# Modulation units of a diffusion backbone: four matmuls of 256 columns on four column groups in place of two of 512 on two

## The chip, the core and the metric

The kernel runs on one core of a Trainium2 chip. The metric is the device time of one execution in microseconds (us): 1765.45 us, the median of three runs (1758.45 to 1767.54). TensorE is called PE here (PEld where it loads weights), VectorE DVE, ScalarE ACT, GpSimd POOL, SyncE SP. SP issues the loads and stores; SPq is its queue.

## What is computed

Two trunk layers work on 640 tokens of 1024 features: 128 context tokens and 512 latent ones. Each layer normalises its input, mixes tokens by three parallel branches (retention, SSD, RG-LRU), and then runs a gated MLP. Both halves of a layer are modulated by a vector that depends on the layer and on the stream (context or latent) alone:

```
sh1, sc1, g1, sh2, sc2, g2 = jnp.split(mod[:, None, :].astype(x.dtype), 6, axis=-1)
h = rmsnorm(x, p['norm1_g']) * (1.0 + sc1) + sh1
mix, new_states = mixer(h, states, p, pos)
x = x + g1 * mix
h = rmsnorm(x, p['norm2_g']) * (1.0 + sc2) + sh2
x = x + g2 * conv_ffn(h, p)
```

Here mod is silu(c) @ w_ada + b_ada, where w_ada has 1024 rows and 6144 columns for each layer. Only the product with w_ada changes; there are two rows of c, one for each stream.

## The kernel before

The products of tokens with weights are split in two: weights and features are each written as a high and a low part (wh, wl and h_hi, h_lo), and three matmuls take the place of one. `Stream` (line 373) loads the weights (tile raw, two buffers), ACT writes wh, and POOL or DVE writes wl. `fm_job` makes products whose output has features on the partitions, `sweep_job` products whose output has tokens there. These jobs stand in one list, the main stream.

The modulation of the first half of layer 0 is made at the start (`start`, tiles ar). The rest is made in five rounds by class `Ada` (line 597): a round covers 2048 columns of w_ada, and has 16 units. A unit is a load of 128 x 1024 weights (tile araw, 512 KB, two buffers) and the matmuls that multiply it with csil, the 128 x 32 piece of silu(c) in which two columns are in use. Since csil is only 32 columns wide, a matmul takes one of the four groups of 32 columns of the array, by its tile_position, and writes 32 partitions of a PSUM tile. Even units (hf = 0) write groups 0 and 1, odd ones (hf = 1) groups 2 and 3. After the sixteenth unit, `finish` (line 643) adds the bias (tile rows), stores the gate's part to DRAM (grow), transposes rows, and writes the shift and the scale.

The order of all instructions is set while the program is built. Everything else (retention, SSD, RG-LRU, norms, `finish`) is a thread that is stepped when its inputs should be there, by a clock of estimated times (class `Clock`, line 60, and `Engine.account`, line 181). The engines run their instructions in the order that comes out. A unit is placed in one of three ways: in `run` (line 349), where the main stream has nothing to issue by that clock; in `Stream.done` (line 411), where more units are left than the rest of the phase should hold; or in `need` (line 682), where the round is due. `run` of Ada returns false as long as the unit's load has not landed by that clock. For the matmuls of a unit the clock has these lines:

```
cost = n * (4 if f32 and fn == "matmul" else 1) / 2400 + 0.003
...
if tp is not None and tp[1] > 0:
    cost = 0.02
```

So a matmul on the first column group is booked by its columns, and one on another group at a small flat price. An even unit is booked dear, an odd one at almost nothing.

In the rows of an order below, a unit is `at<-araw,csil`; `h_hi,wh` and the like are products of the main stream; `ident,tok` and `ident,C` are transposes; `X,wg` are the gates of the RG-LRU (their weights are tile wg); `C`, `pv,C` and `xs,tok` are the SSD's output for one tile of 128 tokens.

Of the kernel before, what the change touches and what calls it, by code (L numbers as in the profile page):

```python
# [59 lines left out]
class Clock:  # L60
    """estimated times of the engines, for the order in which instructions are emitted"""
# [10 lines left out]
    def windows(self, t):  # L72
        """the tensor engine's clock: how busy the last window was sets the rate of the next"""
        while t >= (self.win + 1) * HAM:
            u = self.busy / HAM
            self.cold = u < 0.85 if self.cold else u < 0.33
            self.busy = 0.0
            self.win += 1
# [32 lines left out]
    def free(self, n):  # L111
        """when the last user of a tile is done"""
        return max([r for r in self.read.get(n, {}).values()] + [self.ready.get(n, (0.0,))[0]])
# [20 lines left out]
def tnames(xs):  # L134
    """what the waits go by: tiles, or the rows of the tiles that are worked on in parts"""
    res = []
    for x in xs:
        n = getattr(getattr(x, "tensor", x), "name", None)
        w = ROWS.get(n.rsplit("_", 1)[0]) if n else None
        if w and not n.startswith(SHARED):  # L140
            ap = [(abs(st), c) for st, c in list(x.ap)[1:]]
            o = x.offset
            res += [f"{n}#{r}" for r in range(o // w, (o + sum(st * (c - 1) for st, c in ap)) // w + 1)]
        elif tname(x):
            res.append(n)
    return res


class Slots:
    """a pool whose tiles take over the waits of the tiles that had their place"""  # L150
# [92 lines left out]
def kernel(ctx: ExitStack, tc: tile.TileContext, a: dict, o: dict):  # L243
# [27 lines left out]
    # PSUM tiles and token-major tiles are taken and given back in emission order, so that no engine waits for a later one  # L271
# [91 lines left out]
    def pick(after=0.0, **cost):  # L363
        """the engine that would be through first"""
        return min(cost, key=lambda e: max(clk.t[e], clk.now() - 1.0, after) + cost[e])

# [1 line left out]
    def slot_free(tag, bufs):  # L368
        """when the next tile of the tag is free"""
        L = strm.names.get(tag, [])  # L370
        return clk.free(L[-bufs]) if len(L) >= bufs else 0.0

    class Stream:
        """units of the products' weights: loads run NRAW ahead of the splits, splits tn.look ahead of the products"""
# [56 lines left out]
    def load_x(key, src):  # L431
        """the residual stream stays out of SBUF while the mixer needs the room"""
        pl.enter("xp", key, side="right")
        x[:] = [pl["xp"].tile([128, D], F32, tag=f"x{t}", name="x") for t in range(5)]
        for t in range(5):
            SP.dma_start(x[t], src[t])
# [22 lines left out]
    def softplus(out, xin, n):  # L459
        """max(x, 0) + log1p(exp(-|x|)), log1p through 2 atanh(e / (2 + e))."""  # L460
        e, d, s2, acc = (small(n, f"sp{i}{n}", 1) for i in range(4))
        ACT.activation(e, xin, AF.Abs)
        ACT.activation(e, e, AF.Exp, scale=-1.0)
        yield
        DVE.tensor_scalar(d, e, 2.0, None, ALU.add)
        DVE.reciprocal(d, d)
        DVE.tensor_tensor(e, e, d, ALU.mult)
        DVE.tensor_tensor(s2, e, e, ALU.mult)
        DVE.tensor_scalar(acc, s2, 1.0 / 17.0, 1.0 / 15.0, ALU.mult, ALU.add)
        for c in (13.0, 11.0, 9.0, 7.0, 5.0, 3.0, 1.0):  # L470
            DVE.tensor_tensor(acc, acc, s2, ALU.mult)
            DVE.tensor_scalar(acc, acc, 1.0 / c, None, ALU.add)
        DVE.tensor_tensor(acc, acc, e, ALU.mult)
        DVE.tensor_scalar(d, xin, 0.0, None, ALU.max)
        DVE.scalar_tensor_tensor(out, acc, 2.0, d, ALU.mult, ALU.add)
# [9 lines left out]
    def setup():  # L485
        """log-gates of the retention (l, dir, h), softplus(-lambda) (l, dir, chunk), decay tables"""
# [30 lines left out]
    def fm_job(then, rev=False):  # L517
        """feature-major chunk: then(ps) gives the thread that consumes it"""
        ps = yield from get("mm", 2)
        w = ws.take()  # L520
        for n in range(8):
            for piece in range(2):
                fm_piece(ps, w, (7 - n if rev else n,), piece, 7 if rev else 0)
            if n == 7:
                ws.done()
                spawn(consume(then, ps), 0)
            yield
# [4 lines left out]
    def fm_primed(thens):  # L532
        """some chunks, the columns of the first tiles before the others"""
# [27 lines left out]
    def sweep_job(ks, ncol, ah, al, then, ready=None, keep=None):  # L561
        """token-major product over the k's, units of two k's; then(t, ps) consumes tile t"""
# [32 lines left out]
    mods = {}  # L595

    class Ada:
        """a unit: one k, two slices of 512 of the columns 2048 r .., to rows (32 j + stream)"""
# [19 lines left out]
        def left(self, due):  # L618
            """units up to the round that is due"""
            return max(0, 16 * (1 + ((0, 1), (0, 2), (1, 0), (1, 1), (1, 2)).index(due)) - self.n_run)  # L620

        def run(self):
            """the next unit, if that keeps nobody waiting"""
            if not self.got or clk.ready[tname(self.got[0])][0] > clk.now():
                return False
            l, r, k, hf = self.units[self.n_run]
            if k == 0 and hf == 0:
                if self.busy or not can("at", 1, 2):
                    return False
                self.busy = True  # L630
                self.rows = const.tile([128, 512], F32, tag="rows", name="rows")
                SP.dma_start(self.rows, a["bada"][l, r])
                self.ps, = now_(get("at"))
            raw = self.got.pop(0)
            for j in (2 * hf, 2 * hf + 1):
                PE.matmul(self.ps[32 * j:32 * j + 32, :], csil[:, k, :], raw[:, 512 * (j % 2):512 * (j % 2) + 512],
                          start=(k == 0), stop=(k == 7), tile_position=(0, 32 * j))
            self.n_run += 1
            if k == 7 and hf == 1:
                spawn(self.finish(l, r, self.ps, self.rows))  # L640
            return True

        def finish(self, l, r, ps, rows):
# [3 lines left out]
            if r > 0:  # L647
                j0 = 0 if r == 1 else 2
                dr = dram.tile([2, 1024], F32, tag="grow", name="grow", bufs=4)
                for jj in range(2):  # L650
                    p = 32 * (j0 + jj)
                    SP.dma_start(dr[:, 512 * jj:512 * jj + 512], rows[p:p + 2, :])
# [5 lines left out]
            v = pt.rearrange("p (q j s) -> p q j s", q=4, j=4)  # L658
            which = 0 if r == 0 else 1
            if r < 2:  # L660
                sh = mods["sh", l, which] = const.tile([128, 8, 2], F32, tag=f"sh{which}", name="sh")
                for jj in range(2):
                    DVE.tensor_copy(sh[:, 4 * jj:4 * jj + 4, :], v[:, :, 2 * r + jj, 0:2])
            if r != 1:
                s = const.tile([128, 8, 2], F32, tag=f"s{which}", name="s")
                for jj in range(2):
                    DVE.tensor_scalar(s[:, 4 * jj:4 * jj + 4, :], v[:, :, (2 if r == 0 else 0) + jj, 0:2], 1.0, None, ALU.add)
# [14 lines left out]
    def need(due):  # L682
        """the rounds up to this one, done"""
# [84 lines left out]
    def conv(dst, ps, w, right, rel_):  # L768
        """dst[c] = b + sum_j w[j] ps[c + j - 1]"""
# [17 lines left out]
    def lru(l, c, X, Y, done):  # L787
# [4 lines left out]
        for d in range(2):  # L792
# [22 lines left out]
            DVE.scalar_tensor_tensor(T, r, 1.0, T, ALU.add, ALU.mult)           # 1 - a = (1 + a) tanh  # L815
            DVE.scalar_tensor_tensor(r, T, 2.0, T, ALU.subtract, ALU.mult)      # a^2 - 1
            yield
            ACT.activation(r, r, AF.Sqrt, scale=-1.0)
            ACT.activation(T, T, AF.Identity, scale=-1.0, bias=1.0)             # a
# [36 lines left out]
    def ssd_dt(l, S):  # L856
        """dt, cumulative log-decays and their exponentials, token-major [128, tile, dir, h]"""
# [36 lines left out]
    def ssd_decay(l, S, t):  # L894
        """E[g][m, hh, i]: decay both ways, weighted by dt[m]"""
# [29 lines left out]
    def ssd_state(l, S, C, t):  # L925
        """token-major xs; the states that the chunk leaves, [n, g, (dir, hh, p)]"""
# [105 lines left out]
    def ssd_turn(l, S, t):  # L1032
        """feature-major, with the gain"""
# [33 lines left out]
    def rope_do(raw, t):  # L1067
        """raw -> rotated token-major tile"""
# [186 lines left out]
    def begin_phase(due):  # L1255
        """the modulation that is due at the end of the phase is spread behind its units"""
# [652 lines left out]
```

## Time and profile before

| | |
|---|---|
| runs, median (lowest to highest) | 1765.45 us (1758.45 to 1767.54) |
| profiled execution, own time: its span from first to last instruction | 1752.2 us |
| PE busy | 1661.6 us, 95% |
| DVE, ACT, POOL busy | 1009.3, 718.5 and 537.4 us |
| units of the modulation: PE busy | 53.2 us, between 92.8 and 1197 us |
| granted TensorE clock, mean | 0.982 |

No other time is known for the profiled execution than its span; the median of the runs is 13.2 us above it. A busy time counts the stretch from the start of a matmul to its modelled end, and matmuls are pipelined, so what a matmul costs is read from the start of one to the start of the next. A matmul of plain f32 operands, as the units' are, has two records in the trace; an order has it once.

### The profile page before, as it was taken

To read this page: it belongs to the slowest core of one execution; us is meant where nothing else is said; L and a number is where in the kernel's file an instruction comes from. 1 tells how busy PE (TensorE), PEld (TensorE's weight loads), DVE (VectorE), ACT (ScalarE), POOL (GpSimd) and SP (SyncE) were. 2 spreads that over 40 slices of the span, in tenths; PEclk is the share of its full clock that TensorE was granted. 3 is DMA by queue.
4 is the path that set the end of the run, shared out by engine and by line. 5 is a ranking of instruction groups with operands and counts; after the bars stand their busy time and mean duration, and the time that the engine had idled before them with its cause. 6 is when DMAs were issued, how large, how long until landed. Compare 5 with 4: busy or idle time off the path is not lost.

```text
span 1752.2 us, 25505 instructions
## 1 busy us (share of the span) xinstructions
PE 1661.6 (95%) x10192; PEld 1485.5 (85%) x10192; DVE 1009.3 (58%) x1866; ACT 718.5 (41%) x1136; POOL 537.4 (31%) x344
## 2 busy tenths in 40 slices
PE   6897999999999999999999899999899999999997
PEld 5787878768997999799789876887799989998996
DVE  5467987677443344344464779877854434443445
ACT  6466435426332233223274765443453313331333
POOL 1334653322331233123123355442213212321331
PEclk9998999999999999999999999999999999999999
DMA  8424555533223222322533355643122321222222
GB/s 326 121 49 81 128 179 174 187 109 103 73 73 108 64 82 73 96 73 73 180 121 107 75 135 158 181 166 105 60 73 73 87 81 61 73 85 72 73 85 84
DMA packets 62668, 188.63 MB, mean 108 GB/s; under 512 B 9550, under 2 KB 17734, under 8 KB 62550
## 3 DMA queue, kind: packets, MB, share of 16 engines
q1 hardware_dynamic: 62550, 187.01, 34.7%
q8 instruction: 80, 1.31, 0.3%
q14 instruction: 38, 0.31, 0.1%
HBM read 180.46 MB, written 6.52 MB: 107 GB/s over the span
## 4 chain that ended last, share of the span: by engine, by line
PE 72%; DVE 14%; ACT 4%; DMA 4%; issue 3%; POOL 1%; SPq 0%; POOLq 0%; DVEq 0%; ACTq 0%
PE at L175 72%; DVE tok L175 5%; DVE x L175 2%; DMA wg<-in_wlru 2%; DVE gt L175 1%; DVE sp L175 1%; DVE C L175 1%; DMA tok<-cTd 1%; ACT L175 1%; DVE lb L175 1%; ACT xn L175 1%; ACT hf L175 1%; POOL wl L175 1%; DMA araw<-in_w_ada 1%; ACT lb L175 1%
## 5 line engine op out<-in xcount | busy, mean ns | idle before, releaser
L175 POOL TENSOR_TENSOR wl<-raw,wh 128x1024 fp32r<-128x1024 f32 (+3 forms) x167 | 388.3, 2326 | 946.7 <-ACT wh L175 883.2
L175 PE MATMUL at<-h_hi,wh 128*128 128x258 f32 (+2 forms) x1912 | 599.9, 314 | 5.0 <-ACT wh L175 3.9
L175 PE MATMUL at<-h_hi,wl 128*128 128x258 f32 (+2 forms) x1912 | 590.4, 309 | 5.6 <-POOL wl L175 4.8
L175 PE MATMUL at<-h_lo,wh 128*128 128x258 f32 (+2 forms) x1912 | 590.0, 309 | 0.5 <-DVE h_lo L175 0.5
L175 PEld LDWEIGHTS at<-h_hi,wh 128*128 128x128 f32 x1912 | 363.7, 190 | 20.1 <-issue 5.2
L175 PEld LDWEIGHTS at<-h_hi,wl 128*128 128x128 f32 x1912 | 362.8, 190 | 6.9 <-POOL wl L175 5.9
L175 PEld LDWEIGHTS at<-h_lo,wh 128*128 128x128 f32 x1912 | 364.1, 190 | 2.6 <-DVE h_lo L175 0.7
L175 ACT ACTIVATE wh<-raw 128x1024 fp32r<-128x1024 f32 (+3 forms) x210 | 212.7, 1013 | 223.1 <-PE at L175 168.1
L175 DVE SCALAR_TENSOR_TENSOR cv<-at,par,cv 128x258 f32<-128x258 f32 (+1 forms) x352 | 185.9, 550 | 71.4 <-ACT cv L175 59.6
L175 ACT ACTIVATE cv<-at,par 128x258 f32<-128x258 f32 (+1 forms) x130 | 76.5, 601 | 317.4 <-PE at L175 317.4
L175 PE MATMUL at<-wh,h_hi 128*128 128x384 f32 (+2 forms) x480 | 184.9, 385 | 2.3 <-DVE tok L175 1.4
L175 PE MATMUL at<-wl,h_hi 128*128 128x384 f32 (+2 forms) x480 | 172.6, 359 | 2.7 <-POOL wl L175 2.7
L175 PE MATMUL at<-wh,act_hi 128*128 128x512 f32 x440 | 174.3, 396 | 0.0
L175 PE MATMUL at<-wl,act_hi 128*128 128x512 f32 x440 | 173.6, 395 | 0.6 <-POOL wl L175 0.6
L175 PE MATMUL at<-wh,act_lo 128*128 128x512 f32 x440 | 173.4, 394 | 0.0
L175 PE MATMUL at<-wh,h_lo 128*128 128x384 f32 (+2 forms) x480 | 172.5, 359 | 0.0
L175 DVE TENSOR_SCALAR cv<-at,par 128x384 f32<-128x384 f32 x46 | 31.2, 677 | 188.3 <-PE at L175 188.3
L175 DVE TENSOR_TENSOR gt<-at,gate 128x512 f32<-128x512 f32 x100 | 68.4, 684 | 104.2 <-PE at L175 104.2
L175 ACT ACT_TABLE_LOAD x87 | 111.6, 1283 | 21.9 <-PE at L175 13.6
L175 PEld LDWEIGHTS at<-wh,h_hi 128*128 128x128 f32 x480 | 91.3, 190 | 28.4 <-issue 12.6
L175 PEld LDWEIGHTS at<-wh,act_hi 128*128 128x128 f32 x440 | 82.7, 188 | 24.0 <-issue 3.4
L175 PEld LDWEIGHTS at<-wl,h_hi 128*128 128x128 f32 x480 | 91.2, 190 | 12.2 <-POOL wl L175 3.5
(169 smaller groups left out, 1903.1 us busy)
## 6 DMA issues: line engine op xcount, KB each, us to landing
raw<-in_wup SPq DMA_DIRECT2D x88, 512.0 KB, 3.5
araw<-in_w_ada SPq DMA_DIRECT2D x80, 512.0 KB, 4.5
raw<-in_wdn SPq DMA_DIRECT2D x44, 512.0 KB, 3.5
raw<-in_wfm SPq DMA_DIRECT2D x28, 512.0 KB, 3.6
ar<-in_wada SPq DMA_DIRECT2D x16, 512.0 KB, 10.2
tok<-cTd SPq DMA_DIRECT2D x40, 192.0 KB, 4.6
raw<-in_wout SPq DMA_DIRECT2D x14, 512.0 KB, 3.5
x<-in_xin SPq DMA_DIRECT2D x10, 512.0 KB
```

Of the source, the lines that this page charges most:

```text
L175: res = real(*args, **kw)
```

## The change

Each unit has four matmuls of 256 columns, one on each column group, in place of two of 512 columns on two groups. Even units now fill columns 0 to 255 of the PSUM tile, odd ones 256 to 511. The bias is loaded in eight pieces of 32 x 256 to fit the new layout, the gate's part is stored in four pieces in place of two, and the shift and the scale are copied in one instruction each in place of two. The other lines of the diff take comments away.

```
@@ def run(self):
-                SP.dma_start(self.rows, a["bada"][l, r])
+                src = a["bada"][l, r].rearrange("(h b s) (m c) -> h b m s c", h=2, b=2, m=2)
+                for h_ in range(2):
+                    for b_ in range(2):
+                        for m in range(2):
+                            p = 32 * (2 * b_ + m)
+                            SP.dma_start(self.rows[p:p + 32, 256 * h_:256 * h_ + 256], src[h_, b_, m])
                 self.ps, = now_(get("at"))
             raw = self.got.pop(0)
-            for j in (2 * hf, 2 * hf + 1):
-                PE.matmul(self.ps[32 * j:32 * j + 32, :], csil[:, k, :], raw[:, 512 * (j % 2):512 * (j % 2) + 512],
-                          start=(k == 0), stop=(k == 7), tile_position=(0, 32 * j))
+            for j in range(4):
+                PE.matmul(self.ps[32 * j:32 * j + 32, 256 * hf:256 * hf + 256], csil[:, k, :], raw[:, 256 * j:256 * j + 256],
+                          start=(k == 0 and hf == 0), stop=(k == 7), tile_position=(0, 32 * j), skip_group_check=True)
...
@@ def finish(self, l, r, ps, rows):
-                for jj in range(2):
-                    p = 32 * (j0 + jj)
-                    SP.dma_start(dr[:, 512 * jj:512 * jj + 512], rows[p:p + 2, :])
+                for j in range(4):
+                    SP.dma_start(dr[:, 256 * j:256 * j + 256], rows[32 * j:32 * j + 2, 256 * h_:256 * h_ + 256])
...
-                for jj in range(2):
-                    DVE.tensor_copy(sh[:, 4 * jj:4 * jj + 4, :], v[:, :, 2 * r + jj, 0:2])
+                DVE.tensor_copy(eight(sh), v[:, r, :, :, 0:2])
...
-                for jj in range(2):
-                    DVE.tensor_scalar(s[:, 4 * jj:4 * jj + 4, :], v[:, :, (2 if r == 0 else 0) + jj, 0:2], 1.0, None, ALU.add)
+                DVE.tensor_scalar(eight(s), v[:, 1 if r == 0 else 0, :, :, 0:2], 1.0, None, ALU.add)
```

The planner books every unit alike now, and so the whole order behind the first units comes out another way. Two places in it matter for what follows.

**Place 1** is the end of the mixer of layer 0, on PE, between the last products of the gates (`h_hi,wl`) and the first product of the output projection (`wh,h_hi` of 512 columns). Before:

```order
L175 MATMUL at<-ident,C_634 128x128 x3
L175 MATMUL at<-h_hi,wh 128x258
L175 MATMUL at<-h_lo,wh 128x258
L175 MATMUL at<-h_hi,wl 128x258
L175 MATMUL at<-h_hi,wh 128x384
L175 MATMUL at<-h_lo,wh 128x384
L175 MATMUL at<-h_hi,wl 128x384
L175 MATMUL at<-araw,csil 32x512 x4
L175 MATMUL at<-ident,tok 128x128 x6
L175 MATMUL at<-wh,h_hi 128x512
```

With the change, the same place reads:

```order
L175 MATMUL at<-h_hi,wl 128x384
L175 MATMUL at<-araw,csil 32x256 x8
L175 MATMUL at<-ident,tok 128x128 x9
L175 MATMUL at<-araw,csil 32x256 x24
L175 MATMUL at<-C 128x128 x2
L175 MATMUL at<-pv,C 128x384
L175 MATMUL at<-ident,tok 128x128 x3
L175 MATMUL at<-pv,C 128x384
L175 MATMUL at<-ident,tok 128x128 x3
L175 MATMUL at<-xs,tok 128x64 x6
L175 MATMUL at<-araw,csil 32x256 x16
L175 MATMUL at<-wh,h_hi 128x512
```

Before, two units stood there and the others among products; now twelve units (8, 24 and 16 matmuls, four to a unit) and the SSD's output for its last tile stand between the gates and the output projection.

**Place 2** is in the mixer of layer 1, on PE, between the sweep of z and the product for the second gate of the RG-LRU. Before, this is the whole stretch without a product of the main stream, with a product ahead of it and behind it:

```order
L175 MATMUL at<-wh,h_lo 128x384
L175 MATMUL at<-araw,csil 32x512 x4
L175 MATMUL at<-xs,tok 128x64 x6
L175 MATMUL at<-pv,C 128x384
L175 MATMUL at<-xs,tok 128x64 x6
L175 MATMUL at<-araw,csil 32x512 x2
L175 MATMUL at<-ident,C_8205 128x128 x3
L175 MATMUL at<-araw,csil 32x512 x2
L175 MATMUL at<-h_hi,wh 128x258
```

With the change, this is its first half:

```order
L175 MATMUL at<-wh,h_lo 128x384
L175 MATMUL at<-araw,csil 32x256 x8
L175 MATMUL at<-ident,tok 128x128 x9
L175 MATMUL at<-X,wg 128x258
L175 MATMUL at<-X,wg 128x384
L175 MATMUL at<-ident,C_8322 128x128 x3
L175 MATMUL at<-C 128x128 x2
L175 MATMUL at<-pv,C 128x384
L175 MATMUL at<-X,wg 128x258
L175 MATMUL at<-X,wg 128x384
L175 MATMUL at<-ident,C_8322 128x128 x3
L175 MATMUL at<-araw,csil 32x256 x8
```

Ten more rows of the same kinds follow before the next product: transposes of C (3, then 6 at the end) and of rows (4), two rows of units (4 matmuls each) and the SSD's `C`, `pv,C` and `xs,tok` for what is left of its tiles (2 `C`, 3 `pv,C` and 12 `xs,tok`). The gates `X,wg` of the last direction, which stood 90 rows earlier before, among products, have moved into this stretch, and with them most of the SSD's outputs.

## Rows read from the trace of the kernel before

**Rows 1.** The page: span, and busy time of each engine.

```profile
span 1752.2 us, 25505 instructions
PE 1661.6 (95%) x10192; PEld 1485.5 (85%) x10192; DVE 1009.3 (58%) x1866; ACT 718.5 (41%) x1136; POOL 537.4 (31%) x344
```

**Rows 2.** The page: shares of the chain that ended last, by engine.

```profile
PE 72%; DVE 14%; ACT 4%; DMA 4%; issue 3%; POOL 1%; SPq 0%; POOLq 0%; DVEq 0%; ACTq 0%
```

**Rows 3.** Waits of PE, whole span: waiter, releaser: us, times, longest us.

```profile
PE at L175 <- DMA wg<-in_wlru: 21.7, 4, 11.1
PE at L175 <- DVE tok L175: 13.0, 9, 6.1
PE at L175 <- DMA araw<-in_w_ada: 1.4, 5, 0.5
```

**Rows 4.** Timeline of PE: start us, us, what; one unit, then a pair.

```profile
190.70 1.05 PE L175 MATMUL at<-araw,csil 128*32 128x512 f32 x4
191.68 0.39 PE L175 MATMUL at<-h_hi,wh 128*128 128x258 f32 x1
...
208.76 1.07 PE L175 MATMUL at<-araw,csil 128*32 128x512 f32 x8
209.75 0.44 PE L175 MATMUL at<-wh,h_hi 128*128 128x384 f32 x1
```

**Rows 5.** Timeline of PE in the start: matmuls of 128 columns on four groups.

```profile
32.35 1.95 PE L175 MATMUL at<-ar,csil 128*32 128x128 f32 x64
34.24 0.39 PE L175 MATMUL at<-h_hi,wh 128*128 128x258 f32 x1
...
36.31 1.08 PE L175 MATMUL at<-ar,csil 128*32 128x128 f32 x32
37.32 0.39 PE L175 MATMUL at<-h_hi,wh 128*128 128x258 f32 x1
```

**Rows 6.** Timelines of PE and SPq: a pair, and the next, which waits for its loads.

```profile
328.74 1.06 PE L175 MATMUL at<-araw,csil 128*32 128x512 f32 x8
329.74 0.88 PE L175 MATMUL at<-ident,tok 128*128 128x128 f32 x6
330.37 0.48 PE L175 MATMUL at<-wh,h_hi 128*128 128x512 f32 x1
...
329.83 1.09 SPq L175 DMA_DIRECT2D araw<-in_w_ada  x2
...
333.84 1.05 PE L175 MATMUL at<-araw,csil 128*32 128x512 f32 x4 [0.20 <-DMA araw<-in_w_ada]
335.36 1.05 PE L175 MATMUL at<-araw,csil 128*32 128x512 f32 x4 [0.47 <-DMA araw<-in_w_ada]
```

**Rows 7.** Stretches: us, busy (x instructions) of PE, PEld, DVE, ACT, POOL, granted clock, DMA, GB/s.

```profile
240.00:336.00 96.00, 94.71 (x676) 77.55 (x676) 71.75 (x171) 46.46 (x80) 39.76 (x40) 1.00 0.48 154
1000.00:1120.00 120.00, 111.24 (x636) 91.46 (x634) 99.92 (x211) 70.89 (x119) 64.97 (x64) 0.97 0.55 143
140.00:152.00 12.00, 1.22 (x8) 0.90 (x7) 7.12 (x17) 6.15 (x7) 2.80 (x1) 0.69 0.74 50
152.00:157.00 5.00, 4.71 (x10) 3.16 (x11) 0.00 (x0) 1.59 (x4) 0.00 (x0) 0.50 0.32 120
```

**Rows 8.** Groups of PE matmuls by shape: count, busy us, mean ns, idle before.

```profile
L175 PE MATMUL at<-X,wg 128*128 128x384 f32 x32 | 16.7, 608 | 0.0
L175 PE MATMUL at<-X,wg 128*128 128x258 f32 x32 | 13.7, 520 | 32.1 <-DMA wg<-in_wlru 21.7 <-DVE tok L175 9.9 <-DVE X L175 0.5
L175 PE MATMUL at<-pv,C 128*128 128x384 f32 x32 | 12.8, 498 | 1.7 <-DVE pv L175 0.9 <-DVE tok L175 0.8
L175 PE MATMUL at<-xs,tok 128*128 128x64 f32 x120 | 14.9, 274 | 0.1
L175 PE MATMUL at<-C 128*128 128x128 f32 x40 | 6.1, 278 | 0.0
```

**Rows 9.** SPq's own waits, and the issue of the units' loads (ns min/median/max).

```profile
SPq L175 <- POOL wl L175: 954.3, 151, 22.0
...
L175 SPq DMA_DIRECT2D araw<-in_w_ada x80: 327/333/1583, 48.2 to 1191.4; - x80
```

More of the change, by code (lines that the diff above doesn't have):

```diff
@@ L647, in finish @@
             if r > 0:
-                j0 = 0 if r == 1 else 2
+                h_ = 0 if r == 1 else 1
                 dr = dram.tile([2, 1024], F32, tag="grow", name="grow", bufs=4)
-                for jj in range(2):
-                    p = 32 * (j0 + jj)
-                    SP.dma_start(dr[:, 512 * jj:512 * jj + 512], rows[p:p + 2, :])
+                for j in range(4):
+                    SP.dma_start(dr[:, 256 * j:256 * j + 256], rows[32 * j:32 * j + 2, 256 * h_:256 * h_ + 256])
                 mods["g", l, r] = dr
@@ L657, in finish, with eight @@
             yield
-            v = pt.rearrange("p (q j s) -> p q j s", q=4, j=4)
+            v = pt.rearrange("p (h e j s) -> p h j e s", h=2, e=2, j=4)
             which = 0 if r == 0 else 1
+            def eight(t_):
+                return t_.rearrange("p (j e) s -> p j e s", e=2)
             if r < 2:
                 sh = mods["sh", l, which] = const.tile([128, 8, 2], F32, tag=f"sh{which}", name="sh")
-                for jj in range(2):
-                    DVE.tensor_copy(sh[:, 4 * jj:4 * jj + 4, :], v[:, :, 2 * r + jj, 0:2])
+                DVE.tensor_copy(eight(sh), v[:, r, :, :, 0:2])
             if r != 1:
                 s = const.tile([128, 8, 2], F32, tag=f"s{which}", name="s")
-                for jj in range(2):
-                    DVE.tensor_scalar(s[:, 4 * jj:4 * jj + 4, :], v[:, :, (2 if r == 0 else 0) + jj, 0:2], 1.0, None, ALU.add)
+                DVE.tensor_scalar(eight(s), v[:, 1 if r == 0 else 0, :, :, 0:2], 1.0, None, ALU.add)
                 DVE.tensor_tensor(s, s, P("ng", l, which).unsqueeze(2).to_broadcast([128, 8, 2]), ALU.mult)
```

## The prediction

> **What bounds the kernel now.** I read the page first, then PE's waits, then the units themselves. PE is busy for 1661.6 of 1752.2 us [rows 1], and the chain of work that ended last runs on PE for 72% of the span [rows 2]. So PE is the bound, and its idle time is 90.6 us. Its longest waits are for the weights of the RG-LRU's gates, 21.7 us, and for tiles that DVE writes, 13.0 us; the units' loads cost 1.4 us in all [rows 3]. A change pays here if PE's work shrinks or its waits do. The units lie on PE's path: they stand among products, and in the new form too the next product waits behind them.
>
> **What a unit costs now.** One unit starts at 190.70 and the next product at 191.68: 0.98 us. Two units that follow each other start at 208.76, and the product behind them at 209.75: 0.99 us for both [rows 4]. That is the main finding. An even unit holds column groups 0 and 1, an odd one groups 2 and 3, so two neighbours already run on all four groups at once. The order before has 32 such pairs and 16 single units. With 0.98 and 1.00 us that is 15.7 + 32.0 = 47.7 us.
>
> **What a unit will cost.** The trace has this shape already, in the start, where matmuls of 128 columns go to the four groups in turn. 32 records take 1.01 us (36.31 to 37.32), and 64 take 1.89 us (32.35 to 34.24) [rows 5]. So 32 more records cost 0.88 us, and 0.13 us are fixed for each burst. A unit in the new form is four matmuls of 256 columns, as much streaming as 16 such records: 0.44 us, 0.57 us alone, 1.01 us for two. A single unit wins 0.41 us, a pair nothing. The new order has 12 single units, 29 pairs, a run of six and a run of four: 12 x 0.57 + 29 x 1.01 + 10 x 0.44 + 2 x 0.13 = 40.8 us. **The units' matmuls win 47.7 - 40.8 = 7 us.** From below: if the 0.13 us were paid by each unit of a run, the gain would be 6; it can't pass 80 x 0.41 = 33, and that only if no two units shared the array before.
>
> The rows of the start show no price for more instructions: 32 records cover there what a pair's 8 cover, in 1.01 against 0.99 us [rows 4, 5]. The Trainium skill, TensorEngine Tiling (Array Packing), section Instruction Overhead, speaks against the change here: it gives each matmul some 60 cycles of overhead. My estimate by that page is 25 ns at 2.4 GHz for each of 160 more matmuls, 4 us, and the gain would be 3 us and not 7. The measured 0.02 us for 24 more records decides against it.
>
> **Small parts.** The bias comes in eight pieces, so SP issues 7 more loads in each of five rounds, and 2 more stores in each of four: 43 issues of about 0.33 us, 14 us of SP's queue. I cost them at nothing: SP waits 954 us for POOL to give weight buffers back [rows 9], so it stands idle most of the time ahead of such a load, and a product's weights are loaded well before. Without that cover a burst holds up the weight loads behind it by 7 x 0.33 = 2.3 us, and five bursts cost 12 us. DVE saves six small copies, which change nothing, since DVE is busy for 58% [rows 1].
>
> **What the order costs.** The planner's prices for units changed, and with them the order of everything behind. The order shows two stretches in which PE has no product of the main stream left and must wait for what it gets from others.
>
> Place 1, the end of layer 0's mixer, holds twelve units in a row, with two load buffers. The first pair's loads are there; five more pairs each wait for a buffer, the issue and the landing. The trace has this cycle once: a pair starts at 328.74, SP issues the next loads at 329.83, and PE starts on them at 333.84 and 335.36 [rows 6]. That is 5.1 us from start to start; the first buffer is free 0.4 us earlier now, so 4.7 to 5.1. Five cycles are 23 to 25.5 us, and the last pair's second unit comes 1.5 us later and takes 0.6: 25 to 27.6. DVE gives the same length by another way: I count 57 DVE instructions in the order between the same two products, and in the stretch of 240 to 336 us one takes 71.75 / 171 = 0.42 us [rows 7], so 24 us. I take 26. PE's own work inside: units 5.7 us (1.01 + 6 x 0.44 + 4 x 0.44 + 2 x 0.13), 15 transposes at (330.37 - 329.74) / 6 = 0.105 us, 1.6 us [rows 6], and the SSD's matmuls, by busy time over half their records [rows 8]: 2 C at 0.31, 2 pv,C at 0.80, 6 xs,tok at 0.25, 3.7 us. Together 11. **The wait is 26 - 11 = 15 us.** It is new: PE is idle for 1.3 us in the whole stretch before [rows 7]. Ends: 0, if DVE and the loads are so far ahead on the chip that only the order is odd, and 20, if the loads land late behind the pieces of cTd that SP issues ahead of ten of them.
>
> Place 2, layer 1's mixer, is bound by DVE. The last direction of the RG-LRU and most SSD outputs moved there, and the stretch ends with transposes that need nearly all of it. The order has 67 DVE instructions in it; at 99.92 / 211 = 0.47 us in the stretch of 1000 to 1120 us [rows 7] that is 32 us without a gap. With DVE's busy share there, 0.83, it is 38. PE's own work: six units 3.2, 28 transposes 2.9, four X,wg (two of each shape) 3.8, four pv,C 3.2, four C 1.2, twelve xs,tok 3.0 [rows 6, 8]: 17 us. The wait is 15 to 21; **I take 18 us.** The lower end is about 4: PE's 13.0 us of waits for DVE's tiles [rows 3] lie partly in this mixer, and some may go as this one comes.
>
> The granted clock falls where PE idles. In the stretch of 140 to 152 us PE works 1.2 us and the clock is 0.69; in the 5 us behind it is 0.50, the lower of the two levels (1.2 and 2.4 GHz), and PE does half its work there [rows 7], 2.5 us lost. After two stretches I take 3 us; from 0 (units and transposes keep the clock up) to 6.
>
> **The sum.** -7 + 15 + 18 + 3 = 29 us. The profiled execution's span is 1752.2 us, which becomes 1781; the median of the runs lies 13.2 us above that span, and I keep this: 1781.2 + 13.2 = 1794.4, say **1795 us**, 1.7% slower.
>
> **Rivals.**
>
> The waits are no waits (faster, or no change). The order only looks bare; on the chip DVE, ACT and the loads run ahead of it, and PE finds its inputs. Then the units' 7 us are all that is left: 1758. For it speaks that DVE is busy for only 0.75 of the stretch at place 1 before [rows 7]. Against it speak the two load buffers, which can't run ahead, whatever DVE does. It decides where place 1 takes under 18 us from gates to output projection (11 of work, and a wait as long as the units' gain) and place 2 adds nothing. This is the case on the other side.
>
> Each unit halves and the order is harmless: 80 x 0.41 = 33 us less, 1732. Against it stands the pair at 0.99 us [rows 4].
>
> Both places cost their upper ends. 20 and 21 us, SP's bursts uncovered 12, the clock 6, less 7: 52 us, 1817; with the RG-LRU's weights waiting as long once more as their longest wait, 11.1 us [rows 3], 1828.
>
> It doesn't do what it says: four matmuls of 256 columns pair up two by two. Then a unit takes 0.88 + 0.13 us, 80 units 81 us, 33 more than now, and on top of the order's 36 us the time is 1834. Rows 5 speak against it.
>
> **How the numbers follow.** I give the forecast 0.63, the harmless order 0.14, the upper ends 0.18, the halved units 0.02, the failed concurrency 0.03. The range leaves out the harmless order, the halves and the failed concurrency, 0.19: low 1770, where each place costs about a third, and high 1830, just above the upper ends. A measurement of this kernel tells about 0.5% from no change, 8.8 us: below 1756.6 is faster, above 1774.3 slower. The harmless order at 1758 lies between these, a third of it below: 0.05, with the halves 0.07 faster. The rest of it and the forecast's low end make 0.12 for the same, and 0.81 are left for slower.
>
> **What would show it.** Units: single ones at 0.57 us from start to next product, pairs at 1.01. Place 1: ahead of the first `wh,h_hi` of 512 columns in layer 0, PE idle by about 15 us with waits for araw, and pairs of units some 5 us apart. Place 2: PE idle by 15 us or more ahead of the second gate's product, with DVE's tiles (C, tok, lb) as releasers. PE's busy time falls a little, its idle time grows from 91 to some 125 us. I am wrong if PE's waits for araw stay at a few us, or if the waits in layer 1 shrink as much as place 2 adds.

## The result and the profile after

The change makes the kernel slower: 1804.5 us (median; 1801.59 to 1810.09) against 1763.93 us for the kernel before in the same comparison, a ratio of 1.0241 with a 95% interval of 1.0215 to 1.0267. The forecast was 1795 us in a range of 1770 to 1830, so direction and range held; the loss was sized too small, 29 us of about 41.

The page of the changed kernel, with its span and the busy time of each engine:

```profile
span 1803.2 us, 26214 instructions
PE 1675.1 (93%) x10512; PEld 1510.6 (84%) x10512; DVE 1001.4 (56%) x1855; ACT 724.0 (40%) x1142; POOL 535.6 (30%) x345
```

Against [rows 1], PE's idle time has grown from 90.6 to 128.1 us, where some 125 were forecast. PE's busy time was to fall a little; it has grown by 13.5 us. The mean granted clock fell from 0.982 to 0.965.

Three of PE's waits over the whole span (waiter, releaser: us, times, longest us), to be read against [rows 3]:

```profile
PE at L175 <- DMA wg<-in_wlru: 36.4, 5, 11.9
PE at L175 <- DMA araw<-in_w_ada: 14.6, 10, 3.6
PE at L175 <- DVE tok L175: 13.0, 6, 6.4
```

The units' loads went from 1.4 to 14.6 us, and the weights of the RG-LRU's gates from 21.7 to 36.4. DVE's tile tok has the same sum as before.

A pair of units and the product behind it, in PE's timeline (start us, us, what), to be read against [rows 4]:

```profile
211.30 1.07 PE L175 MATMUL at<-araw,csil 128*32 128x256 f32 x16
212.30 0.44 PE L175 MATMUL at<-wh,h_hi 128*128 128x384 f32 x1
```

A pair takes 1.00 us. In the same timeline a single unit takes 0.57 us to the next instruction (92.78, 185.28 and 276.20), as forecast from the start's rows.

Place 1 in PE's timeline; the bracket is the idle time ahead of an instruction, and what ended it:

```profile
325.29 1.07 PE L175 MATMUL at<-araw,csil 128*32 128x256 f32 x16
326.29 1.20 PE L175 MATMUL at<-ident,tok 128*128 128x128 f32 x9
329.41 0.64 PE L175 MATMUL at<-araw,csil 128*32 128x256 f32 x8 [1.92 <-DMA araw<-in_w_ada]
330.88 0.64 PE L175 MATMUL at<-araw,csil 128*32 128x256 f32 x8 [0.83 <-DMA araw<-in_w_ada]
334.06 1.08 PE L175 MATMUL at<-araw,csil 128*32 128x256 f32 x8 [2.54 <-DMA araw<-in_w_ada]
336.46 1.08 PE L175 MATMUL at<-araw,csil 128*32 128x256 f32 x8 [1.32 <-DMA araw<-in_w_ada]
339.00 1.08 PE L175 MATMUL at<-araw,csil 128*32 128x256 f32 x8 [1.46 <-DMA araw<-in_w_ada]
...
342.29 1.22 PE L175 MATMUL at<-C 128*128 128x128 f32 x4
...
348.09 1.07 PE L175 MATMUL at<-araw,csil 128*32 128x256 f32 x16
352.73 0.80 PE L175 MATMUL at<-araw,csil 128*32 128x256 f32 x8 [3.56 <-DMA araw<-in_w_ada]
...
354.98 0.80 PE L175 MATMUL at<-wh,h_hi 128*128 128x512 f32 x1
```

First units of pairs start at 329.41, 334.06 and 339.00, 4.7 and 4.9 us apart; 4.7 to 5.1 were forecast. The next pair (348.09) comes 9.1 us later: the SSD's output stands ahead of it, 5.8 us of PE's own work from 342.29 on, at a granted clock of 0.66. The stretch took 29.7 us, where 26 were forecast.

Place 2, from its first units to the next product (1155.99), the lines with a wait of over 1 us and the X,wg:

```profile
1114.97 1.07 PE L175 MATMUL at<-araw,csil 128*32 128x256 f32 x16
...
1126.28 2.48 PE L175 MATMUL at<-X,wg 128*128 128x258 f32 x4 [9.10 <-DMA wg<-in_wlru]
1128.55 0.85 PE L175 MATMUL at<-ident,C 128*128 128x128 f32 x3
...
1131.32 1.25 PE L175 MATMUL at<-X,wg 128*128 128x258 f32 x4
1132.41 0.49 PE L175 MATMUL at<-ident,C 128*128 128x128 f32 x3
...
1147.18 2.82 PE L175 MATMUL at<-xs,tok 128*128 128x64 f32 x12 [6.35 <-DVE tok L175]
1151.31 0.88 PE L175 MATMUL at<-ident,C 128*128 128x128 f32 x3 [1.31 <-DVE C L175]
1155.46 0.88 PE L175 MATMUL at<-ident,C 128*128 128x128 f32 x3 [3.28 <-DVE C L175]
```

The releasers C and tok were forecast; the 9.1 us for wg at the head of the stretch were not. What SP issued at that place, and the piece of the chain that is wg's load (start us, us):

```profile
1115.67 0.80 SPq L175 DMA_DIRECT2D araw<-in_w_ada  x2
1116.53 0.42 SPq L175 DMA_DIRECT2D out_lru<-Y  x1
1117.00 9.15 DMA wg<-in_wlru
1117.52 0.85 SPq L175 DMA_DIRECT2D tok<-cTd  x2
```

Here out_lru is a store of the RG-LRU's state, 512 bytes, one element of 4 bytes from each partition. By the updates of their semaphores the two units' loads had landed at 1119.32 and 1120.65. The store took until 1125.97, wg until 1126.15 and the first tok until 1126.33. So wg and tok came with the store, 5.5 us behind the units' loads.

The two X,wg rows show what a wait does to the clock: the same four records take 2.27 us (1126.28 to 1128.55) right behind the wait, and 1.09 us (1131.32 to 1132.41) 5 us later.

**Where the time went, by stage.** The 8496 products of the main stream come in the same sequence in all these kernels, so the start of the n-th one marks the same point of the work in each. With marks at 310.6, 407.3, 957.7, 1087.8, 1095.3 and 1259.2 us of the kernel before (us between marks; one execution each; E are experiments, below):

| | to late in mixer 0 | place 1, output proj. | rest of layer 0 | mixer 1 ahead of place 2 | place 2 | rest of mixer 1 | to the end |
|---|---|---|---|---|---|---|---|
| before | 310.6 | 96.7 | 550.4 | 130.2 | 7.5 | 163.9 | 493.0 |
| after | 310.8 | 111.8 | 549.7 | 142.4 | 41.3 | 154.1 | 493.0 |
| E1: new units, old order | 308.1 | 93.3 | 549.5 | 131.1 | 7.2 | 162.3 | 493.7 |
| E3: layer 0 of after | 308.0 | 112.2 | 549.0 | 132.3 | 6.6 | 164.0 | 493.8 |
| E4: the rest of after | 308.9 | 93.3 | 548.4 | 138.1 | 41.1 | 156.8 | 493.7 |
| E5: after, half loads | 308.0 | 105.7 | 545.6 | 137.7 | 33.6 | 154.6 | 493.3 |
| E6: after, wg early | 296.8 | 111.6 | 547.2 | 132.3 | 39.0 | 154.9 | 493.4 |
| E7: both | 298.7 | 104.7 | 548.6 | 130.8 | 32.9 | 154.3 | 493.5 |
| E10: E1, wg early | 291.5 | 94.6 | 549.3 | 124.0 | 6.5 | 162.9 | 493.9 |

The kernel before had medians of 1763.93, 1756.18, 1753.32 and 1753.97 us in the four comparisons. Times are therefore compared as ratios within a comparison, and traces by stage, best between runs of one chip: E1 to E4 and E7 ran on one, E5, E6 and E10 on another. From before to after the stages add up to 51 us, while the medians are 41 apart; the stages that no edit touches agree within 1 us in the last column and 5 us in the third.

### The profile page after: what moved, and what is told of

Read it like the earlier page. It is cut to its first block, busy times and chain, and to the rows that moved or that the text cites. A ratio compares the mean times of both kernels' runs of the same rounds, so it can differ in the third digit from the quotient of the medians.

```text
span 1803.2 us, 26214 instructions
## 1 busy us (share of the span) xinstructions
PE 1675.1 (93%) x10512; PEld 1510.6 (84%) x10512; DVE 1001.4 (56%) x1855; ACT 724.0 (40%) x1142; POOL 535.6 (30%) x345
## 4 chain that ended last, share of the span: by engine, by line
PE 69%; DVE 14%; DMA 6%; ACT 5%; issue 4%; POOL 2%; SPq 0%; POOLq 0%; DVEq 0%; ACTq 0%
PE at L175 69%; DVE tok L175 5%; DMA tok<-cTd 2%; DVE x L175 2%; DMA wg<-in_wlru 2%; POOL wl L175 1%; DVE sp L175 1%; DMA araw<-in_w_ada 1%; DVE C L175 1%; DVE gt L175 1%; ACT L175 1%; ACT xn L175 1%; ACT hf L175 1%; DVE lb L175 1%; DMA raw<-in_wdn 1%
## 5 line engine op out<-in xcount | busy, mean ns | idle before, releaser
L175 POOL TENSOR_TENSOR wl<-raw,wh 128x1024 fp32r<-128x1024 f32 (+2 forms) x167 | 386.0, 2312 | 1006.9 <-ACT wh L175 967.5
```

The lines of the kernel that those rows point to most:

```text
L175: res = real(*args, **kw)
```

## The experiments

**Order and form taken apart: E1 to E4.** The theory is that the new order costs the time and the new units win a little. The rival is that the new form costs it by itself: twice the matmuls, and 43 more issues on SP. Every step of a unit got two forms, and a switch in the clock of estimated times, so that one form is issued and the other one booked:

```
+    def planned(l, r, step, *args):
+        clk.mode = "real"
+        FORMS[step, REAL](*args)
+        clk.mode = "book"
+        FORMS[step, BOOK(l, r)](*args)
+        clk.mode = None
...
-            for j in range(4):
-                PE.matmul(self.ps[32 * j:32 * j + 32, 256 * hf:256 * hf + 256], csil[:, k, :], raw[:, 256 * j:256 * j + 256],
-                          start=(k == 0 and hf == 0), stop=(k == 7), tile_position=(0, 32 * j), skip_group_check=True)
+            planned(l, r, "mm", self.ps, k, hf, raw)
```

In mode "real" an instruction is issued and not booked, in mode "book" the reverse. The bias loads, the gate's stores and the copies of shift and scale go through it likewise.

E1 issues the new form and books the old one. All engines have the order of before.

> The new units (four matmuls of 256 columns, eight bias loads, four gate stores, single copies), but the planner books the old ones, so that every engine has the order of before. If the order costs all that was lost (theory): only the units' gain is left, about 7 us under the kernel before, 1757 us, ratio 0.996, with PE's waits for araw at some 2 us. If the new form itself costs time (rival: more instructions, more pieces in SP's queue): slower than before, up to about 1800 us.

Measured: 1748.76 us, ratio 0.996 (0.9942 to 0.9977). The page of E1:

```profile
span 1745.2 us, 26189 instructions
PE 1656.6 (95%) x10512; PEld 1495.3 (86%) x10512; DVE 1011.7 (58%) x1860; ACT 719.1 (41%) x1136; POOL 535.4 (31%) x344
```

The new units are a gain, 0.4% or 7 us, with all their matmuls and all 43 issues. So the rival falls.

E2 issues the old form and books the new one.

> The old units (two matmuls of 512 columns on two groups, one bias load), but the planner books the new ones, so that every engine has the order of after. Theory (order): slower than before by as much as the change and by the units' few us more, 1804 to 1812 us, ratio about 1.025, with the waits for araw at the end of layer 0's mixer and for the RG-LRU's weights in layer 1's. Rival (the form costs): about 1764 us, as before.

Measured: 1803.44 us, ratio 1.026 (1.0233 to 1.0287). The old units in the new order are as slow as the change. From E1 to E2, on one chip, are 54.7 us; less the units' 7, the order costs 48 us.

E3 and E4 divide the order: `BOOK` gives "new" for the first two rounds of the modulation (E3), or for the other three (E4).

> The new units; the planner books the new form in the first two rounds of the modulation and the old one in the other three. The stretch at the end of layer 0's mixer (place 1) stands there nearly as in the changed kernel, with twelve units; layer 1's mixer has its old order. If the two places add up (theory): before - 7 + 17 = 1773 us, ratio 1.006. If the loss belongs to layer 1 alone: about 1757. If a late first layer costs more further on: 1790 and more.

Measured: 1767.94 us, ratio 1.0059 (1.0036 to 1.0083).

> The new units; the planner books the old form in the first two rounds and the new one in the other three. Layer 0 has its old order up to the output projection, and layer 1's mixer has the long stretch without products (place 2). If the two places add up (theory): before - 7 + 36 = 1793 us, ratio 1.016. If place 2 is long only because layer 0 came late: about 1757 to 1765.

Measured: 1780.86 us, ratio 1.0133 (1.0109 to 1.0156), against 1.016 expected. Over E1's 0.996, layer 0's order costs 0.010 and layer 1's 0.017, together 0.027; the change costs 0.028. Within these intervals the places add, and the table shows each where it was put (112.2 in the second column of E3, 41.1 in the fifth of E4).

**What holds the two places: E5.** In place 1 the forecast had two causes of one length, the loads' cycle and DVE's 57 instructions. E5 takes the first away. A unit loads half its columns and uses them twice, so half of the modulation's weights are left out, and the room of two buffers holds four; the planner still books whole loads and two buffers.

```
-                t = strm.tile([128, 1024], F32, tag="araw", name="araw", bufs=NADA)
+                t = strm.real.tile([128, 512], F32, tag="araw", name="araw", bufs=4)
...
-                SP.dma_start(t, a["w_ada"][l, 128 * k:128 * k + 128, c:c + 1024])
+                SP.dma_start(t, a["w_ada"][l, 128 * k:128 * k + 128, c:c + 512])
...
-                PE.matmul(self.ps[32 * j:32 * j + 32, 256 * hf:256 * hf + 256], csil[:, k, :], raw[:, 256 * j:256 * j + 256],
+                PE.matmul(self.ps[32 * j:32 * j + 32, 256 * hf:256 * hf + 256], csil[:, k, :], raw[:, 256 * (j % 2):256 * (j % 2) + 256],
```

> The changed kernel with its order, but a unit loads 512 of its 1024 columns (256 KB, not 512) into four buffers that fill the room of the two, and its four matmuls read these columns twice: half of the modulation's weights are left out. Place 1 took 29.7 us from the first unit to the output projection. If the units' loads alone hold it, it falls to about 14 us (11 of PE's own work), and the kernel gains 15 us or more. If DVE holds it as long by itself (DVE is busy for 20.7 us of that stretch), it falls by 4 to 6 us only. In place 2 the loads of tok and wg queue behind 1 MB less: 3 to 5 us. Together some 10 us less than the changed kernel by the second, 1795 us, 20 or more by the first.

Measured: ratio 1.0172 (1.0142 to 1.0202), 0.7% or 12 us under the change, known to some 0.4% either way. Place 1 in E5 goes from its first unit (322.49) to the output projection (346.2): 24 us, and PE waits in it for

```profile
PE at L176 <- DVE tok L176: 6.7, 1, 6.7
PE at L176 <- DMA araw<-in_w_ada: 1.3, 2, 1.0
```

(waits of E5 from 322.2 to 346.3 us). The loads are all but gone as a cause, and the stretch takes 24 us, 6 less than before the edit. That is the length which the forecast gave to its second cause, but it is made up otherwise. DVE is busy for 19.4 us, not for 24. It holds PE until 337.6; the 8.6 us from there on are PE's own work without a gap, at a granted clock of 0.52. Place 2 fell from 41.3 to 33.6 us.

**The RG-LRU's weights: E6.** PE's longest waits after the change are for wg. In place 2 that load stands on SP behind two units' loads of 512 KB and the store out_lru. Ahead of place 2 it stands behind other loads and the same store; SP's timeline from 1009 to 1014 us, and two pieces of the chain there:

```profile
1011.29 0.33 SPq L175 DMA_DIRECT2D raw<-in_wq  x1
1011.67 0.90 SPq L175 DMA_DIRECT2D tok<-cTd  x2
1012.67 0.38 SPq L175 DMA_DIRECT2D out_lru<-Y  x1
1013.14 0.38 SPq L175 DMA_DIRECT2D wg<-in_wlru  x1
```

```profile
1009.44 1.83 POOL wl L175
...
1013.14 8.98 DMA wg<-in_wlru
```

A weight load (raw) waits for POOL to give a buffer back, three others are issued behind it, and only then wg; PE had come to the gate at about 1010. So 3 of its 12 us of waiting lie ahead of the issue, and 9 behind it: raw and tok had landed by 1015.97, out_lru by 1021.92 and wg by 1022.12. E6 loads wg of both directions together, ahead of the first, and books the old place.

```
+        wgs = [fb.tile([128, 2, 128], F32, tag=f"wg{d}", name="wg") for d in range(2)]
+        clk.mode = "real"
+        for d in range(2):
+            SP.dma_start(wgs[d], a["wlru"][l, c, :, d])
+        clk.mode = None
         for d in range(2):
             gates = []
-            wg = fb.tile([128, 2, 128], F32, tag="wg", name="wg")
+            wg = wgs[d]
...
+            clk.mode = "book"
             SP.dma_start(wg, a["wlru"][l, c, :, d])
+            clk.mode = None
```

> The changed kernel with the order of all engines but SP's: the RG-LRU's weights of both directions (wg) are loaded together, ahead of the first direction, into a buffer each. PE waits 36.4 us for wg in the changed kernel, 9.1 of them in place 2 and 11.9 at the start of layer 1's mixer. If these waits are what made layer 1 cost more than DVE's work (theory): 10 to 20 us less, 1785 to 1795, and place 2 falls from 41 to 32 to 36 us. If DVE, or its tiles tok that land beside wg, hold place 2: 0 to 3 us less there.

Measured: ratio 1.0171 (1.0142 to 1.0199), again 0.7% or 12 us under the change. But place 2 fell by 2.3 us only, from 41.3 to 39.0, though its 9.1 us of waiting for wg were gone. The chain of E6 there has the cause:

```profile
1090.13 8.82 DMA tok<-cTd
```

DVE's next tile, tok, is loaded by SP right behind the units' loads and the store out_lru too, and lands as late (out_lru at 1098.79, tok at 1098.95). A wait that is named in the table was not the one that counts; one behind it was as late.

E5 won 7.7 us at this place, and not by the smaller loads. SP's timeline in E5, and the chain's piece for wg:

```profile
1089.68 0.85 SPq L176 DMA_DIRECT2D araw<-in_w_ada  x2
...
1094.92 0.34 SPq L176 DMA_DIRECT2D out_lru<-Y  x1
1095.32 8.02 DMA wg<-in_wlru
```

Both units' loads had landed by 1094.00, ahead of wg's issue, and wg still took 8.0 us behind the store. What changed is the moment of issue. In the changed kernel SP stands at the units' loads until PE gives their buffers back, and issues wg 2.0 us behind the first units of the place; with four buffers it issues it 2.0 us ahead of them.

E7 has both edits.

> The changed kernel's order with both edits: units that load half their columns into four buffers (half of the modulation's weights are left out), and wg of both directions loaded together. If the two act in different places, as their traces say (the first by 6 us in place 1 and 7 in place 2, the second by the first gate's weights in both layers), the gains add: 12 + 12 us, ratio 1.010. Place 2 is then left to DVE and falls to 30 to 33 us. If loads still hold place 2, it stays near 39.

Measured: 1765.04 us, ratio 1.0059 (1.0044 to 1.0074), somewhat better than the sum of both (1.010, itself known to about 0.5%). Place 2 is 32.9 us, near the forecast's 32 us for 67 of DVE's instructions without a gap, but not for that reason. Its windows in E7, up to the landing of tok and from there on (us, busy of PE, PEld, DVE, ACT, POOL, granted clock, DMA share, GB/s):

```profile
1082.80:1088.80 6.00, 5.79 (x44) 3.83 (x42) 1.51 (x4) 5.51 (x12) 2.35 (x3) 1.00 0.77 82
1088.80:1115.70 26.90, 16.32 (x84) 10.32 (x83) 24.32 (x60) 15.91 (x26) 12.32 (x14) 0.68 0.17 56
```

For 6.0 us DVE has next to nothing to do, since tok has not landed; then it is busy for 24.3 of 26.9 us. That second part is much the same in all of them: 29.7 us in the changed kernel, 27.3 in E5, 27.9 in E6. What differs is how long the place waits for its inputs: 11.6, 6.3 and 11.2 us.

**Was the longest wait the cause? E10 and E12.** E6 won most of its time outside place 2: in layer 0 (296.8 us, where the runs without its edit have 308 to 311) and ahead of place 2 (132.3, where the new order without it has 137.7 to 142.4). If the new order had made those waits, the old order would win less by the same edit. E10 is E1 with that edit, E12 is the kernel before with it.

> The new units in the order of before, with wg of both directions loaded together. PE waits 25.9 us for wg in that kernel without this. If half of the waits go and nothing takes their place: about 12 us less, ratio to the kernel before 0.989. If other inputs come as late: no gain, 0.996.

Measured: 1725.64 us, ratio 0.9846 (0.9817 to 0.9875).

> The kernel before with the one edit that wg of both directions is loaded together; the units stay two matmuls of 512 columns. If the new units and the early loads add up: 20 us less than before, ratio 0.989 (0.985 with the new units). If the early loads help only in the new form: 1.000.

Measured: 1735.16 us, ratio 0.9889 (0.9873 to 0.9906). The old order gains 1.1%, 20 us, at least as much as the new one with its 12. So the wait for wg, the longest of the table, is a loss of both orders. With the edit in both, the stretch ahead of place 2 still differs by 8.3 us (132.3 and 124.0, on one chip), without it by 7.0 (138.1 in E4 and 131.1 in E1, on one chip). In E6 other waits stand there: PE's waits from 955.5 to 1087.8 us are

```profile
PE at L176 <- DVE C L176: 5.2, 2, 4.7
PE at L176 <- ACT xs L176: 4.2, 1, 4.2
PE at L176 <- DVE tok L176: 3.5, 2, 2.6
PE at L176 <- DMA araw<-in_w_ada: 1.8, 1, 1.8
```

No single one of them is as long as 8 us. Which of them one would have to mend is open.

E10 beats both kernels. Its gain is that of the units (0.9846 / 0.9889, 0.4%) and of the early loads, and the two add. That it gains without any change of order is what the store out_lru lets expect: behind it wg lands late in every order. No run moves the store itself.

**Would the right price have helped? E9.** E9 books each unit at what a single one takes on the chip.

```
-            if tp is not None and tp[1] > 0:
-                cost = 0.02
+            if tp is not None:
+                cost = 0.1425 if n == 256 else 0.02 if tp[1] > 0 else cost
```

> The new units, each booked at 0.57 us, what one costs alone on the chip, not 0.49. The order has again ten units in place 1, and place 2 grows to 27 rows with ten units. If only the order counts: as slow as the changed kernel within 15 us, 1790 to 1820. If the planner needs only a right price: 1757.

Measured: ratio 1.0286 (1.0263 to 1.0309). The better price gives an order that is as slow; its place 2 takes 61.3 us, and the mixer ahead of it 118.7. By the lines quoted from the clock, an even unit was booked at 0.876 and an odd one at 0.04, 0.92 for both; the new pair is booked at 0.98. The sum hardly moved, only its distribution did, and everything behind came out in another way.

## Why the prediction was right in its direction and short in its size

**The units, -7 us: right.** Pairs at 1.00 and singles at 0.57 us are in the trace, and E1 gained 7 us by the median. The Trainium skill, TensorEngine Tiling (Array Packing), section Instruction Overhead, gives each matmul some 60 cycles; by my estimate from that page the gain would have been 3 us. The rows of the units show no such price here: 8 matmuls of a pair take 1.00 us, as 4 did.

**The small parts at nothing: right.** E1 has all 43 issues and the eight-piece bias, and keeps the 7 us.

**Place 1, 15 us: somewhat too small.** The units' gain is counted apart, so the place is compared with E1: E3, on the same chip, has 18.9 us more in this column. The cycle of two buffers is as forecast, and E5 shows that it held the place. But the SSD's output on PE was taken to run beside the cycles; it stands between two of them and makes the stretch 29.7 us, not 26. That DVE alone gave the same length holds for the sum only: in E5 a third of the 24 us is PE's own work at the lower clock.

**Place 2, 18 us: too small.** The column grew by 33.8 us, of which 9.8 come back in the next one, since the work was moved: 24 net; E4 against E1, on one chip, has 28.4 (33.9 less 5.5). The step that failed is "bound by DVE", from the start of the place and "without a gap". DVE's part is 27 to 30 us, in which it is busy for 23 to 24, and not 32; that E7 takes 32.9 is luck. What was left out are the 11.6 us until tok and wg land. They are issued late, since SP stands at the units' loads until PE frees their buffers, and land some 9 us after their issue, right behind the store out_lru. The forecast looked at the count of DVE's instructions, and not at what SP issues ahead of their inputs. That the store causes the late landing is read from the order of the landings in these traces; no run took it away.

**Ahead of place 2, nothing: missed.** The forecast said that the order shows two stretches. There the mixer of layer 1 lost another 12.2 us in this pair of traces, and 7.0 in E4 against E1 on one chip, without any long stretch bare of products. The table of waits offers wg for it; E6 and E10 show that this wait was there in both orders, and that some 8 us stay when it is gone. What causes them is open.

**The clock, 3 us (0 to 6): too small.** E1 and the changed kernel issue the same instructions, in 10512 records on PE each. PE's busy time is 1656.6 us in one and 1675.1 in the other, and its idle time 88.6 and 128.1. So of 58 us, 39.5 are idle, where 33 were forecast, and 18.5 are work that takes longer. E3 and E4, which ran on E1's chip, give nearly the same together: 38.0 idle and 17.9 of longer work. The rows of X,wg above show such work at half speed. In place 1 PE was busy for 16.4 us where 11 were forecast, at a granted clock of 0.74; the forecast's 3 us counted only the first products behind each place. No run held the clock up, so how much of the 18.5 us would be saved by that is not shown.

**From span to median, +13.2 us: not a term.** The changed kernel's profiled execution took 1804.95 us, 1.75 more than its span. So only about 2 us lie around a span; the rest of the 13.2 was that the profiled execution of before was a quicker one. In spans the sum was 29 and the difference 51; in medians 29 and 41. The addition hid a part of the miss.

**The rivals.** The harmless order is out by E2, the halved units and the failed concurrency by the rows of the units. The upper ends came nearest: the loads that land late were in that case, though it put them at place 1, behind pieces of cTd, and into waits for wg.

## What to carry to other kernels

Where a planner sets the order, an edit has two effects, and they can be measured apart: issue one form and book the other. An edit whose own effect is a few us can be lost many times over by the order that its price brings, and a truer price need not bring a better one. For a stretch without the bound engine's work, count the instructions of the engine that feeds it, but look as well at what stands ahead of that engine's inputs in the load queue, where a store of 512 bytes can count for more than loads of 512 KB; and before a long wait is called the cause, take it away in both kernels.

## What the runs showed of the hardware

The store out_lru, 512 bytes in 128 elements of 4 bytes, took 6.6 to 10.3 us from its issue to the last update of its semaphore (94 stores in the twelve traces; for two more, updates are missing). A load of wg, 128 KB, that was issued within 1.5 us behind such a store landed 6.4 to 12.4 us after its issue (38 loads). Without such a store in the 12 us ahead of it, it took 3.2 to 5.0 us (33 loads). In place 2 of the changed kernel the last packet of wg had ended at 1121.08, and the last update of its semaphore came at 1126.15, 0.18 us behind the store's: PE waited 5 us for data whose packets were through.

Behind a wait of 9 us PE ran at the lower of its two levels, in the middle of a busy mixer. The windows of the changed kernel over the two X,wg rows shown above:

```profile
1126.30:1128.50 2.20, 2.20 (x4) 1.35 (x5) 2.02 (x7) 0.25 (x1) 0.00 (x0) 0.50 0.03 7
1131.30:1132.80 1.50, 1.50 (x8) 0.96 (x6) 1.43 (x6) 1.49 (x3) 0.92 (x1) 1.00 0.00 0
```

The granted clock is 0.50 in the first and 1.00 in the second.
